# A macaron transformer layer in split fp32: idle-time products, a later normalise, paired copies and an earlier rounding

## The chip, the cores and the metric

The kernel runs on one core of a Trainium2 chip. The time is device time in microseconds from the first to the last instruction of one execution; three executions of the kernel before gave 1914.36, 1914.66 and 1914.83 us (median 1914.66). One further execution was recorded by the profiler: 1912.22 us, of which the trace covers a span of 1910.4 us.

## The reference

One layer of a decoder: a half-step SwiGLU FFN, a token mixer (differential attention beside an S5 state space model), and a second half-step FFN. Each block modulates its input with a shift and a scale that come from a condition vector `c`, and ends in a residual sum and a layer norm. There are 256 tokens, the model width is 2048, all arrays are fp32.

```python
mod = (silu(c) @ w_cond + b_cond)            # 3 blocks x (shift, scale, gate) x 2048
u = x * (1 + scale0) + shift0
h = (silu(u @ w1) * (u @ w3)) @ w2           # first FFN
x = layer_norm(alpha * x + 0.5 * (1 + gate0) * h)
u = x * (1 + scale1) + shift1
q, k, v, s = split(u @ w_in)                 # 4 x 1024 columns
h = concat(diff_attention(q, k, v), s5(s)) @ w_out
x = layer_norm(alpha * x + (1 + gate1) * h)
u = x * (1 + scale2) + shift2
h = (silu(u @ w1b) * (u @ w3b)) @ w2b        # second FFN
x = layer_norm(alpha * x + 0.5 * (1 + gate2) * h)
```

## The kernel before

**Tiles and jobs.** The weights are streamed from DRAM in tiles of 128x1024 fp32. One tile is one job, and the jobs come in a fixed order: 264 of the first FFN, 104 of the mixer (16 s jobs, 32 for q and k, 16 for v, 8 for the gate of the S5 output, 32 of the output product), 264 of the second FFN. Each tile `raw` is split into two rounded parts: `hi` by a cast on ScalarE (line 691), `lo = raw - hi` on VectorE. Activations are split in the same way (`Uh`, `Ul`; `Hh`, `Hl`). TensorE multiplies three times, hi·Uh, hi·Ul and lo·Uh, and adds up in PSUM. A raw tile is loaded by SyncE's queue up to four tiles ahead; `hi` and `lo` have rings of four.

**Order.** The program is written straight through: `Stream.run` emits for each job the products, then what hangs on the job (`post`, and what was put off with `later`), then the split of the tile four jobs on, then `drain`. Each engine works off its own instructions in the order in which they were emitted. `drain` fills VectorE: it keeps a model clock for VectorE (`V.t`) and TensorE (`PE.t`) and emits background work while `V.t` is less than `lim` ahead of `PE.t`. The background work is of two kinds: `gv` steps (one multiply-and-sum of a 128x1024 tile of `w_cond`, 258 of them in all) and the preparation of the S5 tables (`tabc`, `tabr`, `cells`). From job 70 of the first FFN until its end `lim` is 3.0.

**The kosum jobs.** In the first FFN, part of the sums over the input width is kept in SBUF (`kosum`) and completed later; in jobs 70 to 96 VectorE adds these up beside the splitting. From there on a group of up-projection jobs ends with `sg`, the product of silu and the other half, whose transposes TensorE makes next.

**The two turns.** Between blocks, the layer norm is computed per token half t (128 tokens): VectorE gathers the statistics, then `normalise(q)` scales a quarter of 512 columns, on ScalarE for t=0 and on VectorE for t=1 (table `NOW`, all four quarters at once). `turn(ks, then)` transposes Y by TensorE (`ps<-ident,Y`, 128 columns each, twice two for each of the eight pairs `k2`), and `put` makes u from the transposed tile: the scaled copy `uf` and every second `Uh` on ScalarE, the others and `Ul` on VectorE. The first turn covers k2 = 0 and 1, which the first job needs; the others follow one by one between products or jobs. Below, T2 to T7 are the transposes of pairs 2 to 7. T4 and T5 read quarter 2 of Y, T6 and T7 quarter 3.

**The s jobs.** Jobs of the mixer 0 to 7 take half 0 of the input width, 8 to 15 half 1, for the eight tiles t of s. Two tiles share one PSUM buffer. After a job of half 1 ScalarE copies the tile to `sT` (line 1147) and issues its DMA to `sD` in DRAM (line 1150); after t=3 and t=7 GpSimd loads four such tiles back in the layout of the scan (`U<-sD`, line 1156). The scan's first products (`ps<-U,s5e`) come at `S5_AT` = job 17.

Nearly all VectorE and TensorE instructions carry the line of the recording helper (L106), so the rows below are told apart by their tiles.

Of the kernel before, what the change touches and what calls it, by code (L numbers as in the profile page):

```python
# [10 lines left out]
F32R = mybir.dt.float32r  # L11
# [6 lines left out]
T = 256  # L18
# [15 lines left out]
AHEAD = 4  # L34
# [5 lines left out]
LIM = (3.0, 100.0, 100.0, 100.0)  # L40
GVM = (0.57, 0.65, 0.85, 0.4)
LAG = 8.0
S5_WAIT = 1.7
BG_AT = 70
GV_END = 256
GA = (20, 24)
UNITS = ([("p", 0, q) for q in range(4)] + [("g", 2, h) for h in range(2)] + [("p", 3, q) for q in range(4)]
# [2 lines left out]
O_AT = (61, 69)  # L50
H_AT = 21
AV_AT = (57, 65)
S5_AT = 17
S5_STEP = 4
X_AT = (239, 240, 244, 250)
Z_AT = (242, 246, 251, 256)
NOW = (4, 4)
QUIET = 3
RW = (8, 3, 64)
MAGIC = 12582912.0  # L60
# [57 lines left out]
def tile_layer(tc, A, out):  # L118
    nc = tc.nc
    V, S, PE, SP, GP = Meter(nc.vector), nc.scalar, Meter(nc.tensor), nc.sync, nc.gpsimd  # L120
    with ExitStack() as ctx:
        sb = ctx.enter_context(tc.tile_pool(name="sb", bufs=1))
# [7 lines left out]
        def psum():  # L130
            return psp.tile([128, 512], F32, tag="ps", name="ps")
# [7 lines left out]
        def w1(shape, name):  # L139
            return small(shape, name, 5, tag="w1")  # L140
# [16 lines left out]
        SP.dma_start(sc[0:1, :], A["c"])  # L157
        ident = sb.tile([128, 128], F32, tag="ident", name="ident")
        make_identity(nc, ident)
        mask = sb.tile([128, 384], F32, tag="mask", name="mask")  # L160
        GP.memset(mask, 0.0)
        for c0 in (0, 256):
# [27 lines left out]
        for q in range(4):  # L190
            p, cs = psum(), slice(q % 2 * 512, q % 2 * 512 + 512)
# [9 lines left out]
        sD = dram.tile([1024, 4, 64], F32, tag="sD", name="sD")  # L201
        yD = dram.tile([1024, 4, 64], F32, tag="yD", name="yD")

        st = {"raw": RAW, "split": 2, "lim": None, "gv_max": 0.0, "gv_credit": 0.0, "s5_at": 0.0}

        gv_order = [(u, kt) for u in UNITS for kt in range(NS)]
# [22 lines left out]
        def gv_step():  # L231
            n = gv_n["done"]
            gv_load(n + (8 if n < GV_RING else GVB))
            t = gv_tiles.pop(n)
            u, j = gv_order[n]
            if j == 0:
                st["acc"] = small([128, NS], "acc")
                if n < GV_RING:
                    V.memset(st["acc"], 0.0)
            w = t.shape[-1]  # L240
            gv_n["done"] += w // 1024
            if n == 0:
                st["shift"] = p = psum()[:, 0:1]
                for k in range(NK):
                    PE.matmul(p, t[:, k * 128:(k + 1) * 128], scT[:, k:k + 1], start=k == 0, stop=k == NK - 1)
            else:
                c0 = 0 if w > 1024 else j % 2 * 1024
                V.scalar_tensor_tensor(out=t, in0=t, scalar=1.0, in1=sc[:, c0:c0 + w], op0=ALU.mult, op1=ALU.mult,
                                       accum_out=st["acc"][:, j:j + 1])
                pay_late()  # L250
            n, j = gv_n["done"] - 1, j + w // 1024 - 1
            if n < 4 * NS and j % 8 == 7:
                finish(u, st["acc"], j // 4 - 1, j // 4 + 1)
            elif n >= 4 * NS and j == NS - 1:
                gv_end(u, st.pop("acc"))
# [476 lines left out]
        stream = Stream()  # L732
# [146 lines left out]
            for x, n in zip(st["gb"], ("lng", "lnb")):  # L879
                SP.dma_start(x[:, cs], A[n][sub:sub + 1, cs].to_broadcast([128, 1024]))  # L880

        def turn(ks, then):

            ps = {}
            for k2 in ks:
                for t in range(2):
                    st.pop(("norm", k2 // 2, t), lambda: None)()
            for t in range(2):
                for k2 in ks:
                    if t == 0:  # L890
                        ps[k2] = psum()
                    for i in range(2):
                        PE.transpose(ps[k2][:, i * 256 + t * 128:i * 256 + (t + 1) * 128],
                                     st["Y"][t][:, (2 * k2 + i) * 128:(2 * k2 + i + 1) * 128], ident)
                    if t == 1:
                        then(k2, ps[k2])

        def turn_mod(blk):
            def then(k2, p):
                gv_until("ready", blk, k2 // 2)  # L900
                for i in range(2):
                    k = 2 * k2 + i
                    put(kx(st["U"][0], k), kx(st["U"][1], k), p[:, i * T:(i + 1) * T],
                        GS[blk][:, k:k + 1], BT[blk][:, k:k + 1], i)
            return then
# [211 lines left out]
        def mixer():  # L1117
            jobs = []
            M = {}
# [10 lines left out]
            def mk_s(t, hf):  # L1130
                def mm(hi, lo):
                    if hf == 0 and t % 2 == 0:
                        M["ps", t // 2] = psum()
                    M["pt"] = p = M["ps", t // 2][:, (t % 2) * T:(t % 2 + 1) * T]
                    for k in range(8):
                        between(8 * hf + k)
                        w = hi[:, k * 128:(k + 1) * 128]
                        PE.matmul(p, w, kx(st["U"][0], 8 * hf + k), start=hf == 0 and k == 0 and t % 2 == 0,
                                  stop=False, skip_group_check=True)
                        PE.matmul(p, w, kx(st["U"][1], 8 * hf + k), start=False, stop=False, skip_group_check=True)  # L1140
                    for k in range(8):
                        PE.matmul(p, lo[:, k * 128:(k + 1) * 128], kx(st["U"][0], 8 * hf + k), start=False,
                                  stop=hf == 1 and k == 7, skip_group_check=True)

                def post():
                    s = w1([128, 4, 64], "sT")
                    S.copy(s, M["pt"].rearrange("p (c i) -> p i c", i=4))  # L1147
                    if t % 2:
                        M.pop(("ps", t // 2))
                    S.dma_start(sD[t * 128:(t + 1) * 128], s)  # L1150
                    if t % 4 == 3:
                        h = t // 4
                        if h == 0:
                            M["U4"] = slab("U4")
                        for i in range(4):
                            GP.dma_start(
                                M["U4"][32 * i:32 * i + 32, h * 1024:(h + 1) * 1024]
                                .rearrange("p (g c) -> p g c", c=64),
                                sD[h * 512:(h + 1) * 512, i, :].rearrange("(g p) c -> p g c", p=32))
                return Job(mm, halves(A["win_a"][t], hf), post if hf else None)  # L1160
# [392 lines left out]
        stream.q[RW[2]].pre.append(lambda: st.update(raw=RAW))  # L1553
        stream.run(BG_AT)
        bg5.extend(fill)
        n0 = stream.done
        st["gv_due"] = lambda n: 64 + 96.0 * (n - n0) / (GV_END - n0)
        st["lim"], st["gv_max"] = LIM[0], GVM[0]
        stream.run(4 * NT1 - BG_AT)
        bg5.extend(rest)  # L1560
        new_stats()
        stream.run(len(parts[0]) - 4 * NT1 - QUIET)
# [6 lines left out]

        st["X"] = st["Y"]  # L1570
        st["U"] = pairs("U")
        turn(range(2), turn_mod(3))
        mid[2] = lambda: turn((2,), turn_mod(3))
        mid[4] = lambda: turn((3,), turn_mod(3))
        for i in range(4):
# [15 lines left out]
        def kept(k2, p):  # L1591
            q = k2 // 2
            S.copy(xT[:, (k2 % 4) * 512:(k2 % 4 + 1) * 512], p)
            if k2 % 2:
                st["xT", 6, q] = xT[:, (q % 2) * 1024:(q % 2 + 1) * 1024]
                if ("ready", 6, q) in st:
                    modulate(6, q)
        turn(range(2), turn_mod(6))
        stream.later(0, lambda: turn((2,), turn_mod(6)))
        stream.later(1, lambda: turn((3,), turn_mod(6)))  # L1600
        for i in range(4):
# [77 lines left out]
```

## Time and profile before

| | |
|---|---|
| median of three executions | 1914.66 us |
| profiled execution | 1912.22 us, span 1910.4 us |
| TensorE matmuls busy | 1858.5 us, 97% of the span |
| VectorE busy | 1488.1 us, 78% |
| ScalarE busy | 889.4 us, 47% |
| DMA | 532 MB, mean 279 GB/s |
| mean granted clock of TensorE | 0.989 of full speed |

TensorE is the engine to watch: what is not its own work shows up as idle time ahead of a matmul, written in the timeline as `[idle <- what ended it]`. The end of a matmul is modelled, so the distance between two starts tells more than a duration does. The clock column of a window is the mean granted clock in parts of full speed (2.4 GHz); 0.50 is the lower level of 1.2 GHz.

### The profile page before, as it was taken

How to read it: one execution, taken by the hardware profiler on the slowest of the kernel's cores; microseconds unless marked ns; L12 is line 12 of the kernel's file. 1: busy time of each engine (PE TensorE's matmuls, PEld its weight loads, DVE VectorE, ACT ScalarE, POOL GpSimd, SP SyncE). 2: the span in 40 equal slices, each digit the busy share in tenths (PEclk: the TensorE clock that was granted, in tenths of full speed). 3: DMA queues.
4: the chain of work that ended last, by engine and by line, in shares of the span. 5: the costliest groups of instructions: out<-in, count | busy, mean ns of one | idle time of the engine just before them, and what ended most of it. 6: DMA issues, size and time to landing. Idle time of an engine off the chain costs nothing.

```text
span 1910.4 us, 25429 instructions
## 1 busy us (share of the span) xinstructions
PE 1858.5 (97%) x9326; PEld 1567.5 (82%) x9326; DVE 1488.1 (78%) x2255; ACT 889.4 (47%) x1211; POOL 65.0 (3%) x119
## 2 busy tenths in 40 slices
PE   6999999999999999899999998999999999999996
PEld 5888878888888888889999886888888888888885
DVE  6889899978888979888998987887876555445468
ACT  3544444465445433634457635544444444344442
POOL 0000000000000000111210000000000000000000
PEclk9999999999999999999999998999999999999998
DMA  9999878889899888798988885998887555565563
GB/s 375 363 338 315 296 247 292 295 306 309 305 347 326 308 323 312 280 337 294 313 268 311 283 309 202 339 357 275 294 279 249 187 188 191 194 215 187 191 233 110
DMA packets 151935, 532.36 MB, mean 279 GB/s; under 512 B 21841, under 2 KB 23297, under 8 KB 150657
## 3 DMA queue, kind: packets, MB, share of 16 engines
q1 hardware_dynamic: 137234, 495.32, 74.3%
q0 software_dynamic: 6512, 23.89, 3.7%
q10 hardware_dynamic: 8064, 11.54, 1.7%
q8 instruction: 73, 1.20, 0.2%
q14 instruction: 52, 0.43, 0.1%
HBM read 513.34 MB, written 17.33 MB: 278 GB/s over the span
## 4 chain that ended last, share of the span: by engine, by line
PE 87%; DVE 6%; DMA 4%; ACT 2%; issue 1%; POOL 0%; SPq 0%; DVEq 0%; ACTq 0%; POOLq 0%
PE ps L106 87%; DVE lo L106 2%; DVE Y L106 2%; DMA raw<-in_f1w_dram 1%; DVE gv L106 1%; ACT hi L691 1%; DMA early<-in_w_cond_dram 1%; DMA raw<-in_wout_dram 0%; DMA U<-sD 0%; DVE st L106 0%; DVE r L106 0%; DMA sD<-sT 0%; DMA early<-in_wc_dram 0%; ACT Y L865 0%; DVE early L106 0%
## 5 line engine op out<-in xcount | busy, mean ns | idle before, releaser
L106 DVE TENSOR_TENSOR lo<-raw,hi 128x1024 fp32r<-128x1024 f32 x630 | 766.3, 1222 | 342.1 <-ACT hi L691 338.5
L691 ACT CAST hi<-raw 128x1024 fp32r<-128x1024 f32 x630 | 661.4, 1053 | 705.8 <-PE ps L106 461.0
L106 PE MATMUL ps<-hi,Uh 128*128 128x512 f32 x1472 | 583.7, 397 | 16.7 <-ACT Uh L318 9.7
L106 PE MATMUL ps<-hi,Ul 128*128 128x512 f32 x1472 | 577.5, 392 | 0.8 <-DVE Ul L106 0.8
L106 PE MATMUL ps<-lo,Uh 128*128 128x512 f32 x1472 | 457.4, 392 | 1.3 <-DVE lo L106 1.3
L106 PEld LDWEIGHTS ps<-hi,Uh 128*128 128x128 f32 x1472 | 278.7, 189 | 77.8 <-ACT Uh L318 10.4
L106 PEld LDWEIGHTS ps<-lo,Uh 128*128 128x128 f32 x1472 | 278.4, 189 | 60.9 <-DVE lo L106 2.0
L106 PEld LDWEIGHTS ps<-hi,Ul 128*128 128x128 f32 x1472 | 279.0, 190 | 58.1 <-DVE Ul L106 1.9
L106 DVE SCALAR_TENSOR_TENSOR gv<-gv,sc 128x1024 f32<-128x1024 f32 x258 | 314.2, 1219 | 1.4 <-DMA gv<-in_w_cond_dram 1.3
L106 PE MATMUL ps<-hi,Hh 128*128 128x512 f32 (+1 forms) x716 | 274.6, 385 | 0.0
L106 PE MATMUL ps<-hi,Hl 128*128 128x512 f32 (+1 forms) x716 | 273.6, 383 | 0.0
L106 PE MATMUL ps<-lo,Hh 128*128 128x512 f32 (+1 forms) x716 | 216.5, 384 | 1.8 <-DVE lo L106 1.8
L106 PEld LDWEIGHTS ps<-lo,Hh 128*128 128x128 f32 x716 | 133.0, 188 | 29.1 <-DVE lo L106 2.6
L106 PEld LDWEIGHTS ps<-hi,Hh 128*128 128x128 f32 x716 | 134.5, 188 | 26.8 <-issue 0.4
L106 PEld LDWEIGHTS ps<-hi,Hl 128*128 128x128 f32 x716 | 134.6, 188 | 26.0
L106 PE MATMUL ps<-Uh,hi 128*128 128x256 f32 x384 | 97.9, 292 | 2.4 <-ACT sT L1147 1.8
L106 PE MATMUL ps<-Ul,hi 128*128 128x256 f32 x384 | 95.7, 286 | 0.1
L106 PEld LDWEIGHTS ps<-Uh,hi 128*128 128x128 f32 x384 | 74.2, 193 | 6.2 <-ACT sT L1147 2.7
L106 PEld LDWEIGHTS ps<-Ul,hi 128*128 128x128 f32 x384 | 74.2, 193 | 0.8 <-DVE Ul L106 0.7
L1010 ACT CAST Hh<-ps 128x512 fp32r<-128x512 f32 x44 | 25.8, 587 | 78.6 <-PE ps L106 78.6
L106 PE MATMUL ps<-Uh,lo 128*128 128x256 f32 x384 | 53.9, 283 | 0.0
L106 DVE TENSOR_TENSOR Hl<-ps,Hh 128x512 fp32r<-128x512 f32 x44 | 30.3, 688 | 30.0 <-ACT Hh L1010 29.7
(229 smaller groups left out, 1393.4 us busy)
## 6 DMA issues: line engine op xcount, KB each, us to landing
raw<-in_f1w_dram SPq DMA_DIRECT2D x264, 512.0 KB, 6.0
raw<-in_f2w_dram SPq DMA_DIRECT2D x264, 512.0 KB, 4.7
gv<-in_w_cond_dram SPq DMA_DIRECT2D x258, 512.0 KB, 7.1
raw<-in_win_a_dram SPq DMA_DIRECT2D x48, 512.0 KB, 6.0
raw<-in_wout_dram SPq DMA_DIRECT2D x32, 512.0 KB, 5.8
early<-in_w_cond_dram SPq DMA_DIRECT2D x28, 512.0 KB, 7.6
s5m<-scrB POOLq DMA_DIRECT2D x8, 1024.0 KB, 8.4
raw<-in_win_v_dram SPq DMA_DIRECT2D x16, 512.0 KB, 4.8
```

The source lines that it names most:

```text
L106: return f(*a, **k)
L691: S.copy(hi, raw)
L1010: S.copy(hh, p)
```

## The change

- `LIM_KO` = 1.5 takes the place of 3.0 as `lim` for jobs 70 to 96; after these it is 3.0 as before.
- `S5_AT` is 18 in place of 17: the scan's loads and products come one job later.
- `NOW` = (4, 1): for t=1, VectorE normalises only quarter 0 at once. Quarter 1 follows right behind the first turn, quarters 2 and 3 at the start of the turns of T4 and T6.
- `warm(n)` emits n products 128x512 of a small constant tile `wr` into a PSUM buffer that nobody reads: 20 after the first shift product at the opening; 11 after the t=0 transposes and 3 after the t=1 transposes of the mixer's first turn; 12 and 3 at the second FFN's.
- The s copies wait for the odd tile and are then made for both.
- In the second FFN, `split_to(done + AHEAD, False)` right behind the first turn emits the casts of the next three tiles there.

```diff
@@ constants
+LIM_KO = 1.5
-S5_AT = 17
+S5_AT = 18
-NOW = (4, 4)
+NOW = (4, 1)
+WARM = dict(opening=20, mixer=(11, 3), ffn=(12, 3))
@@ tile_layer
+        wr = sb.tile([128, 32], F32R, tag="wr", name="wr")
+        V.tensor_copy(wr, ident[:, 0:32])
...
+        def warm(n):
+
+            p = psum()
+            for _ in range(n):
+                PE.engine.matmul(p, wr[:, 0:1].to_broadcast([128, 128]), wr.unsqueeze(1).to_broadcast([128, 16, 32]), start=True, stop=True)
...
                     PE.matmul(p, t[:, k * 128:(k + 1) * 128], scT[:, k:k + 1], start=k == 0, stop=k == NK - 1)
+                warm(WARM["opening"])
@@ turn
-        def turn(ks, then):
+        def turn(ks, then, idle=(0, 0)):
...
                     if t == 1:
                         then(k2, ps[k2])
+                if idle[t]:
+                    warm(idle[t])
@@ mk_s
                 def post():
-                    s = w1([128, 4, 64], "sT")
-                    S.copy(s, M["pt"].rearrange("p (c i) -> p i c", i=4))
-                    if t % 2:
-                        M.pop(("ps", t // 2))
-                    S.dma_start(sD[t * 128:(t + 1) * 128], s)
+                    if t % 2 == 0:
+                        return
+                    p = M.pop(("ps", t // 2))
+                    for i in range(2):
+                        s = w1([128, 4, 64], "sT")
+                        S.copy(s, p[:, i * T:(i + 1) * T].rearrange("p (c i) -> p i c", i=4))
+                        S.dma_start(sD[(t - 1 + i) * 128:(t + i) * 128], s)
                     if t % 4 == 3:
@@ main program
-        st["lim"], st["gv_max"] = LIM[0], GVM[0]
+        st["lim"], st["gv_max"] = LIM_KO, GVM[0]
         stream.run(4 * NT1 - BG_AT)
+        st["lim"] = LIM[0]
         bg5.extend(rest)
...
-        turn(range(2), turn_mod(3))
+        turn(range(2), turn_mod(3), WARM["mixer"])
+        st.pop(("norm", 1, 1))()
         mid[2] = lambda: turn((2,), turn_mod(3))
...
-        turn(range(2), turn_mod(6))
+        turn(range(2), turn_mod(6), WARM["ffn"])
+        st.pop(("norm", 1, 1))()
+        stream.split_to(stream.done + AHEAD, False)
         stream.later(0, lambda: turn((2,), turn_mod(6)))
```

VectorE near the end of the first FFN's up-projections, before: the second S5 table is finished here (`tabc<-tabc,tabr 128x16x32` are its last two operations), and then there are only splits and `gv` steps.

```order
L106 TENSOR_TENSOR lo<-raw,hi 128x1024
L106 SCALAR_TENSOR_TENSOR gv,acc<-gv,sc 128x1024
L106 TENSOR_TENSOR tabc<-tabc,tabr 128x16x32
L106 TENSOR_TENSOR lo<-raw,hi 128x1024
L106 SCALAR_TENSOR_TENSOR gv,acc<-gv,sc 128x1024
L106 TENSOR_TENSOR lo<-raw,hi 128x1024
L106 TENSOR_TENSOR tabc<-tabc,tabr 128x16x32
L106 TENSOR_TENSOR lo<-raw,hi 128x1024
L106 SCALAR_TENSOR_TENSOR gv,acc<-gv,sc 128x1024
L106 TENSOR_TENSOR lo<-raw,hi 128x1024 x2
```

The same last operations in the changed program. The first `lo` of this piece is split 241 of the stream; in the piece above the first is split 231.

```order
L108 TENSOR_TENSOR lo<-raw,hi 128x1024
L108 SCALAR_TENSOR_TENSOR gv,acc<-gv,sc 128x1024
L108 TENSOR_TENSOR tabc<-tabc,cells 128x32x32
L108 TENSOR_TENSOR lo<-raw,hi 128x1024
L108 TENSOR_TENSOR tabr<-tabc,cells 128x1024
L108 TENSOR_TENSOR lo<-raw,hi 128x1024
L108 SCALAR_TENSOR_TENSOR gv,acc<-gv,sc 128x1024
L108 TENSOR_TENSOR sg<-sg,ps 128x512 x2
L108 TENSOR_TENSOR lo<-raw,hi 128x1024
L108 TENSOR_TENSOR tabc<-tabc,tabr 128x16x32
L108 TENSOR_TENSOR lo<-raw,hi 128x1024
L108 SCALAR_TENSOR_TENSOR gv,acc<-gv,sc 128x1024
```

The last table operations have moved some ten splits later, past the last `sg` of the up-projections.

VectorE at the mixer's first turn, before, from the four normalises of t=1 (`Y<-Y,mv,rs`) on; the last `CAST Uh` here belongs to T4.

```order
L106 TENSOR_SCALAR Y<-Y,mv,rs 128x512 x4
L106 CAST Uh<-uf 128x256
L106 TENSOR_TENSOR Ul<-uf,Uh 128x256 x2
L106 CAST Uh<-uf 128x256
L106 TENSOR_TENSOR Ul<-uf,Uh 128x256 x2
L106 TENSOR_TENSOR lo<-raw,hi 128x1024
...
L106 TENSOR_TENSOR lo<-raw,hi 128x1024 x4
L106 SCALAR_TENSOR_TENSOR gv,acc<-gv,sc 128x1024
L106 CAST Uh<-uf 128x256
```

The same stretch in the changed program; the third normalise is that of quarter 2, which T4 reads.

```order
L108 TENSOR_SCALAR Y<-Y,mv,rs 128x512
L108 CAST Uh<-uf 128x256
L108 TENSOR_TENSOR Ul<-uf,Uh 128x256 x2
L108 CAST Uh<-uf 128x256
L108 TENSOR_TENSOR Ul<-uf,Uh 128x256 x2
L108 TENSOR_SCALAR Y<-Y,mv,rs 128x512
L108 TENSOR_TENSOR lo<-raw,hi 128x1024
...
L108 TENSOR_TENSOR lo<-raw,hi 128x1024 x4
L108 SCALAR_TENSOR_TENSOR gv,acc<-gv,sc 128x1024
L108 TENSOR_SCALAR Y<-Y,mv,rs 128x512
L108 CAST Uh<-uf 128x256
```

Three of the four normalises have moved back; quarter 2 now stands behind four splits and a `gv` step, and quarter 3 two splits and another `gv` step further on.

VectorE at the second FFN's first turn in the changed program, from the normalise of quarter 1 to that of quarter 2 and the `gv` step behind it. Before, a single `lo` stood ahead of T2's `CAST Uh` here, four behind it, and no normalise among them.

```order
L108 TENSOR_SCALAR Y<-Y,mv,rs 128x512
L108 TENSOR_TENSOR lo<-raw,hi 128x1024 x4
L108 CAST Uh<-uf 128x256
L108 TENSOR_TENSOR Ul<-uf,Uh 128x256 x2
L108 TENSOR_TENSOR lo<-raw,hi 128x1024
L108 CAST Uh<-uf 128x256
L108 TENSOR_TENSOR Ul<-uf,Uh 128x256 x2
L108 TENSOR_TENSOR lo<-raw,hi 128x1024
L108 SCALAR_TENSOR_TENSOR gv,acc<-gv,sc 128x1024
L108 TENSOR_SCALAR Y<-Y,mv,rs 128x512
L108 TENSOR_TENSOR lo<-raw,hi 128x1024
L108 SCALAR_TENSOR_TENSOR gv,acc<-gv,sc 128x1024
```

The four splits have come forward past T2's put, and the normalise of quarter 2 stands behind a split and a `gv` step.

## Rows read from the trace of the kernel before

**Rows 1.** page, chain that ended last: share of the span by engine
```profile
PE 87%; DVE 6%; DMA 4%; ACT 2%; issue 1%; POOL 0%; SPq 0%; DVEq 0%; ACTq 0%; POOLq 0%
```

**Rows 2.** TensorE's waits: us in total, times, longest
```profile
PE ps L106 <- ACT Uh L318: 9.7, 2, 7.6
PE ps L106 <- DVE Y L106: 6.3, 2, 3.2
...
PE ps L106 <- DVE kosum L106: 3.3, 3, 1.2
...
PE ps L106 <- ACT sT L1147: 1.8, 4, 0.5
```

**Rows 3.** timeline, TensorE at the opening: start, us, engine, operation, [idle before]
```profile
38.86 0.74 PE L106 MATMUL ps<-hi,Uh 128*128 128x512 f32 x1 [2.09 <-ACT Uh L318]
```

**Rows 4.** timeline, VectorE in a kosum period
```profile
266.75 1.28 DVE L106 TENSOR_TENSOR kosum<-ps,kosum 128x512 f32<-128x512 f32 x2
```

**Rows 5.** timeline, VectorE in the last up-projections and TensorE beside it
```profile
712.69 1.22 DVE L106 TENSOR_TENSOR lo<-raw,hi 128x1024 fp32r<-128x1024 f32 x1 [2.15 <-ACT hi L691]
...
718.75 1.28 DVE L106 TENSOR_TENSOR sg<-sg,ps 128x512 f32<-128x512 f32 x2
...
720.26 0.60 PE L106 MATMUL ps<-ident,sg 128*128 128x128 f32 x4
...
773.97 0.72 PE L106 MATMUL ps<-lo,Hh 128*128 128x512 f32 x2 [1.20 <-DVE lo L106]
```

**Rows 6.** windows: length, busy PE, PEld, DVE, ACT, POOL, clock, DMA
```profile
714.00:774.00 60.00, 58.80 (x276) 48.83 (x274) 58.68 (x84) 25.55 (x25) 0.00 (x0) 1.00 0.85 303
787.50:792.50 5.00, 4.42 (x19) 3.85 (x17) 4.61 (x12) 4.11 (x9) 2.05 (x4) 0.50 0.98 353
1152.50:1167.50 15.00, 10.86 (x26) 7.74 (x27) 8.73 (x15) 7.25 (x12) 0.00 (x0) 0.50 0.20 66
```

**Rows 7.** timeline, VectorE and TensorE at the start of the mixer
```profile
786.11 2.04 DVE L106 TENSOR_SCALAR Y<-Y,mv,rs 128x512 f32<-128x512 f32 x4
788.07 0.28 DVE L106 CAST Uh<-uf 128x256 fp32r<-128x256 f32 x1
...
795.01 4.64 DVE L106 TENSOR_TENSOR lo<-raw,hi 128x1024 fp32r<-128x1024 f32 x4 [0.52 <-ACT hi L691]
799.57 1.22 DVE L106 SCALAR_TENSOR_TENSOR gv<-gv,sc 128x1024 f32<-128x1024 f32 x1
...
802.60 1.22 DVE L106 TENSOR_TENSOR lo<-raw,hi 128x1024 fp32r<-128x1024 f32 x1
...
786.71 1.11 PE L106 MATMUL ps<-ident,Y 128*128 128x128 f32 x4 [3.06 <-DVE Y L106]
...
798.60 0.60 PE L106 MATMUL ps<-ident,Y 128*128 128x128 f32 x4
...
805.23 0.60 PE L106 MATMUL ps<-ident,Y 128*128 128x128 f32 x4
```

**Rows 8.** timeline, the s tiles' way to the scan: ScalarE's queue, GpSimd, TensorE
```profile
831.17 0.33 ACTq L1150 DMA_DIRECT2D sD<-sT  x1
...
838.16 2.59 POOL L1156 DMA_DIRECT2D U<-sD  x4 [46.89 <-ACT sT L1147]
...
848.87 1.97 PE L106 MATMUL ps<-U,s5e 128*128 128x64 f32 x16 [2.30 <-DMA U<-sD]
```

**Rows 9.** timeline, TensorE and ScalarE at the start of the second FFN
```profile
1156.25 1.22 PE L106 MATMUL ps<-lo,Uh 128*128 128x512 f32 x2 [1.27 <-DVE lo L106]
...
1163.38 0.79 PE L106 MATMUL ps<-hi,Uh 128*128 128x512 f32 x1 [2.49 <-ACT hi L691]
...
1169.07 0.47 PE L106 MATMUL ps<-hi,Uh 128*128 128x512 f32 x1
...
1178.33 0.60 PE L106 MATMUL ps<-ident,Y 128*128 128x128 f32 x4
...
1162.29 3.88 ACT L691 CAST hi<-raw 128x1024 fp32r<-128x1024 f32 x4
```

More of the change, by code (lines that the diff above doesn't have):

```diff
@@ L1133, in mm @@
                         M["ps", t // 2] = psum()
-                    M["pt"] = p = M["ps", t // 2][:, (t % 2) * T:(t % 2 + 1) * T]
+                    p = M["ps", t // 2][:, (t % 2) * T:(t % 2 + 1) * T]
                     for k in range(8):
```

## The prediction

> **What bounds the kernel now.** The chain of waits comes first: 87% of it is TensorE [rows 1], so the kernel is bound by the products, and only time in which TensorE stands still or runs at the lower clock can be gained. The list of TensorE's waits then says how much there is: 9.7 us in two waits for ScalarE's Uh, 6.3 in two for VectorE's Y, 3.3 in three for kosum, 1.8 in four for the sT copy [rows 2]. Each is followed up in the timeline, engine beside engine, and the granted clock is read in windows around them. The lower level of 1.2 GHz (0.50) holds for 5 us at the mixer's start and for 15 us at the second FFN's [rows 6]. Every part of the change touches one of these places, and each is small: their sum is what decides.
>
> **The opening.** The 20 unread products stand in the first long wait, 7.6 us [rows 2]. What one costs comes from the second FFN: from 1163.38 to 1169.07 lie 13 times 512 columns, 0.44 us each at the lower level; from 1169.07 to 1178.33 lie 38, 0.24 each [rows 9]. Twenty take 4.9 to 8.8 us, so at worst they end 1.2 late. What would be gained by a faster clock behind them is lost again: after jobs 0 to 3 TensorE waits 2.09 us for the next Uh [rows 3], which hangs on loads and conditions and not on TensorE. The same wait hides the 1.2. Value 0, bounds -0.8 (the waits behind 2.09 shrink a little) and +1.2.
>
> **LIM_KO.** Each kosum wait ends on the sum at 266.75 [rows 4], which stands behind a lo and a gv step. The order of the changed kernel keeps that gv step and takes away the one of the earlier split, where VectorE isn't late. I take 0.1 of the 3.3 us; bounds 0 and 3.3. What is deferred comes back later: the last four table operations now stand behind splits 241, 242, 244 and 245. At VectorE's durations for such sizes, 1.22 for 1024 elements (the lo rows) and 0.64 for 512 (two sg in 1.28) [rows 5], they are 2 x 1.22 + 2 x 0.64 = 3.7 us. Before them VectorE has idle time, as the 2.15 at 712.69 shows [rows 5]. Behind them it has not: from 714 to 774 it is busy for 58.7 of 60 us [rows 6], and TensorE ends that stretch waiting 1.20 for lo [rows 5]. So 3.7 less the 1.3 idle, +2.4, appears there, part of it already at 720.26, where the transposes start 0.2 to 0.3 behind the end of sg [rows 5]. Bounds: 0, if VectorE had got further ahead by then, and 3.7. The part: +2.3.
>
> **The mixer's turn.** The four normalises took 2.04 us from 786.11, and the first CAST Uh followed at 788.07 [rows 7]. But that CAST also needs ScalarE's uf, which needs the transposes at 786.71; at best it starts 1.3 us after these, so hardly earlier than now. The later normalising gains 0.1 here. What is late next are T2, T4 and T6. T2 reads quarter 1, which now stands behind the first four Ul: about 0.4 net, since ScalarE's puts are the pace there. T4 was reached at 798.60. Quarter 2 stands behind the four lo from 795.01 and the gv step from 799.57, and takes 2.04 / 4 = 0.51: 799.57 + 1.22 + 0.51 = 801.3, a new wait of 2.7 us. T6 was reached 6.63 us after T4. VectorE needs between T4 and T6: 1.36 until the CAST (from 786.71 to 788.07), 1.9 for the put and the small operations (from the gv step's end near 800.7 to 802.60), a lo of 1.16, a gv step of 1.22, a put of some 1.2, a lo of 1.16 and the normalise of 0.51, in all 8.5 [rows 7]. That is 1.9 of new wait. Eleven products of 0.24 fill 2.7 of the 3.06 us at 786.71, so the clock may stay up there instead of at 0.50 for 5 us; but that stretch goes at the pace of the puts, VectorE 4.61 and ScalarE 4.11 busy of 5.00 [rows 6], and I take 0.5 for it. Together -0.1 + 0.4 + 2.7 + 1.9 - 0.5 = +4.4. Bounds +1.5 (T6 not late, a full gain of the clock) and +7 (the clock falls in the new wait of 2.7, as it did in the one of 3.06, and costs half of another 5 us).
>
> On this point the Trainium skill (Perfetto Trace Analysis, the part on how TensorE's profile differs) says that ScalarE, VectorE and GpSimd are strictly first in, first out. By that rule the normalise cannot pass the lo and gv rows, and the two waits stand; were it otherwise, the part would be about 0 and the sum 4.6 us lower.
>
> **The s tiles.** TensorE waited four times 0.45 for a copy of the tile whose buffer it needed [rows 2]; with copies only after the odd tile the next job has another buffer: -1.8. The loads of the scan: sD is issued at 831.17, GpSimd issues U from 838.16, TensorE waits 2.30 until 848.87 [rows 8]. Now one more copy and issue stand ahead, 0.45 + 0.33 = 0.8 later; TensorE gets there a job later, half of 6.63 less a turn's 0.4 [rows 7], 2.9 us, less the two waits of 0.45 that vanish in between. The wait becomes 2.30 + 0.8 - 2.9 + 0.9 = 1.1: -1.2. Together -3.0; bounds -1.8 and -4.1.
>
> **The second FFN's turn.** Job 1 started at 1163.38 after 2.49 us for a hi whose casts ScalarE began only at 1162.29 [rows 9]. Now three are cast before. The first lo, awaited until 1156.25, moves back by one normalise, to 1156.75. From there job 0 has 8 products and T2 left, 9 x 512 columns: at 0.24 to 0.44 each job 1 starts at 1158.9 to 1160.7, and job 2 (13 x 512 on) at 1162.1 to 1166.4, where it was at 1169.07 [rows 9]: a gain of 7.0 at full clock, 2.7 at the lower level, 5.6 if the clock comes back early in job 1. The last is what I take, since TensorE still stands 2.75 us before 1156.75. Then T4: from T3 on, ScalarE needs 1.7 for the put (1.36 to VectorE's CAST [rows 7], and its own last cast) and 3.88 / 4 = 0.97 for the hi, VectorE 1.16 + 1.22 + 0.51, in all 5.6 against 13 x 0.24 = 3.2: a new wait of 2.4. T6 stands behind lo, gv, lo, gv: 1.7 by the same sums. Together -5.6 + 2.4 + 1.7 = -1.5; bounds -4.5 and +1.5.
>
> **The sum.** 0 + 2.3 + 4.4 - 3.0 - 1.5 = +2.2 us on the profiled execution of 1912.2 us, 1914.4. The median of the runs lies 2.4 above that execution, so 1916.9; with the clock's side a little kinder in both turns than the middle of my bounds, I put down 1916.5.
>
> **Rivals.**
> 1. *The clock is the main thing.* The products keep 2.4 GHz through both turns: the 15 us at 0.50 [rows 6] hold 10.9 us of matmul, of which half, 5.4, comes back, 7.0 with the earlier start; the mixer gives back 2.2 of its 4.42. The new waits are shorter because VectorE is ahead: 3.5 in all for T4 and T6 of both turns. -3.0 - 7.0 - 2.2 + 3.5 + 1.0 (tables) = -7.7: about 1907. For it: the gap of 3.06 is nearly filled. Against it: the puts set the pace, and the new waits are as long as some that stood before. The Trainium skill (TensorE: Matmul & The Clock Gate, "What's actually happening") has the low level as the default that activity lifts; by it the unread products should hold the clock, which the rows of the kernel before can't show, as nothing fills the gaps there.
> 2. *The late normalises lower the clock again.* The new waits of 2.7 and 2.4 at T4 each drop it, as the one of 3.06 ahead of 786.71 was followed by 0.50 [rows 6, 7]. Against it: after the wait of 2.30 the 16 products of 64 columns took 1.97 us [rows 8], no sign of a lower level, and the new waits lie between the two. It decides once the windows behind T4 show 0.50 at all. Price 2.5 each, half of the mixer's 5 us: +2.2 + 5.0, on the scale of the median 1922.
> 3. *The shorter limit does what it says.* The three kosum waits go and the tables find room: -3.3 - 2.3 instead of +2.3: 2.2 - 5.5, about 1911.
>
> **Chances.** The forecast, with a spread of 3 us, 0.50; rival 1 0.18; rival 2 0.20; rival 3 0.12. The measurement tells about 0.2%, 3.8 us, from no change: faster is below 1910.8, slower above 1918.5. Faster: 0.16 of rival 1, 0.05 of rival 3, 0.03 of the forecast, 0.24. Slower: 0.18 of rival 2 and 0.11 of the forecast, 0.29. The same: 0.47. The range of 8 in 10 leaves out the lower half of rival 1 and the upper half of rival 2: 1908 to 1922.
>
> **What will show it.** Idle times ahead of the transposes of T4 and T6 in both turns, ended by VectorE's Y: 2.7, 1.9, 2.4, 1.7. No wait for sT and one near 1.1 for U. Waits for sg or lo near 720 and 774 that are 2.4 us longer in sum. The kosum waits still 3 and 3.2 us. Job 1 of the second FFN near 1159 relative to the lo that ends the wait of 1156. I am wrong if T4 starts without a wait, if the windows of the turns show a clock near 1.00 throughout with TensorE the pace, or if VectorE's tables fit before 714.

## The result, and the profile after

The changed kernel takes 1924.45 us (median of six executions, 1919.88 to 1930.91) against 1914.74 for the kernel before, measured beside it: a ratio of 1.0051, 95% interval 1.0031 to 1.0070, so 6 to 13 us slower. The forecast was 1916.5. Single executions of one kernel lie up to 8 us from their median (1907.36 to 1919.64 around 1914.87 in 26 executions of the kernel before), so times below come with their interval, and a single trace is read for where the time goes.

The profiled execution of the changed kernel, the fastest of its six, has a span of 1918.1 us. The page's chain of waits, which was 87% TensorE before [rows 1]:

```profile
PE 80%; DVE 9%; DMA 5%; ACT 3%; issue 2%; ACTq 1%; POOL 0%; SPq 0%; DVEq 0%
```

TensorE's share fell by seven points, VectorE's rose from 6% to 9%. The list of TensorE's waits (total, times, longest):

```profile
PE ps L108 <- DVE Y L108: 9.9, 7, 2.4
PE ps L108 <- DVE lo L108: 6.0, 4, 2.5
PE ps L108 <- ACT Uh L329: 4.8, 2, 4.0
...
PE ps L108 <- DVE kosum L108: 3.2, 3, 1.1
PE ps L108 <- DMA U<-sD: 3.1, 1, 3.1
PE ps L108 <- DVE s5e L108: 2.6, 3, 1.4
```

The waits for sT are gone and the opening's waits for Uh have shrunk from 9.7 to 4.8 us [rows 2], as the 20 unread products now stand in the first of them. Waits for Y have grown from two to seven, for lo from 3.6 to 6.0 us in sum, and there are three for s5e that did not stand there before. The timeline of TensorE shows the places, each with the idle time ahead:

```profile
38.29 0.50 PE L108 MATMUL ps<-hi,Uh 128*128 128x512 f32 x1 [3.96 <-ACT Uh L329]
...
755.86 0.73 PE L108 MATMUL ps<-lo,Hh 128*128 128x512 f32 x2 [0.80 <-DVE lo L108]
...
773.25 0.73 PE L108 MATMUL ps<-lo,Hh 128*128 128x512 f32 x2 [1.94 <-DVE lo L108]
...
790.71 0.44 PE L108 MATMUL ps<-ident,Y 128*128 128x128 f32 x2 [1.25 <-DVE Y L108]
...
801.27 0.44 PE L108 MATMUL ps<-ident,Y 128*128 128x128 f32 x2 [2.32 <-DVE Y L108]
...
809.49 0.44 PE L108 MATMUL ps<-ident,Y 128*128 128x128 f32 x2 [1.38 <-DVE Y L108]
...
853.77 2.43 PE L108 MATMUL ps<-U,s5e 128*128 128x64 f32 x16 [3.11 <-DMA U<-sD]
...
999.74 0.77 PE L108 MATMUL ps<-s5e,s5m 128*128 128x64 f32 x4 [1.39 <-DVE s5e L108]
...
1164.76 0.72 PE L108 MATMUL ps<-lo,Uh 128*128 128x512 f32 x2 [2.46 <-DVE lo L108]
...
1177.43 0.44 PE L108 MATMUL ps<-ident,Y 128*128 128x128 f32 x2 [2.38 <-DVE Y L108]
...
1185.56 0.44 PE L108 MATMUL ps<-ident,Y 128*128 128x128 f32 x2 [1.48 <-DVE Y L108]
```

At 38.29 the opening's second wait is 3.96 us in place of 2.09 [rows 3]: what the earlier jobs gained is waited off here. 755.86 and 773.25 are lo waits near the end of the first FFN, 2.7 us in place of 1.20 [rows 5]. 790.71, 801.27 and 809.49 are T2, T4 and T6 of the mixer, 1177.43 and 1185.56 T4 and T6 of the second FFN. 853.77 is the scan's first product, 999.74 a product of a later batch of the scan.

To see where the time went, the trace is cut at instructions that both kernels have: the first kosum transposes, the first transposes of the mixer's turn, T7, the scan's first product, the first transposes of the second FFN's turn, its T7, the last product. In us, from one trace of each kernel:

| stretch | before | changed | difference |
|---|---|---|---|
| start to kosum | 247.9 | 246.3 | -1.6 |
| kosum to the mixer's turn | 535.2 | 536.0 | +0.9 |
| the mixer's turn, to T7 | 25.5 | 30.3 | +4.9 |
| T7 to the scan's first product | 40.3 | 41.1 | +0.8 |
| scan's first product to the second FFN's turn | 298.6 | 301.9 | +3.3 |
| the second FFN's turn, to T7 | 34.1 | 32.9 | -1.2 |
| T7 to the last product | 714.5 | 715.2 | +0.7 |

The fourth and fifth stretch belong together, because the scan begins one job (2.9 us) later: together +4.1.

The granted clock in windows (third number from the end; the first five pairs are the busy times of TensorE, its weight loads, VectorE, ScalarE, GpSimd):

```profile
787.50:792.50 5.00, 3.49 (x19) 2.15 (x17) 4.58 (x10) 3.42 (x8) 1.81 (x4) 1.00 0.97 329
800.00:805.00 5.00, 3.73 (x32) 3.73 (x33) 3.60 (x14) 2.38 (x4) 0.00 (x0) 1.00 0.89 267
853.00:855.50 2.50, 1.73 (x14) 1.76 (x15) 0.85 (x3) 1.05 (x1) 0.00 (x0) 0.92 1.03 414
855.50:858.00 2.50, 2.50 (x13) 2.50 (x13) 0.61 (x1) 0.00 (x0) 1.86 (x3) 0.50 1.03 419
858.00:860.50 2.50, 2.50 (x21) 2.50 (x20) 0.13 (x1) 1.05 (x1) 1.28 (x3) 0.90 1.02 413
1002.50:1005.00 2.50, 2.50 (x8) 2.03 (x8) 2.43 (x7) 0.48 (x3) 0.00 (x0) 0.50 0.95 277
1165.00:1167.50 2.50, 2.50 (x8) 1.83 (x8) 2.50 (x3) 0.49 (x1) 0.00 (x0) 0.65 0.64 179
```

In the mixer's turn the clock now stays at 1.00 where it was 0.50 [rows 6], also behind the wait of 2.32 (800 to 805). Behind the 3.11 us for U it falls to 0.50, behind the 1.39 us for s5e to 0.50 (1002.5 to 1005), and behind the 2.46 us for lo in the second FFN to 0.65.

### The profile page after: what moved, and what is told of

Read it like the earlier page. It is cut to its first block, busy times and chain, and to the rows that moved or that the text cites. A ratio compares the mean times of both kernels' runs of the same rounds, so it can differ in the third digit from the quotient of the medians.

```text
span 1918.1 us, 25529 instructions
## 1 busy us (share of the span) xinstructions
PE 1868.0 (97%) x9375; PEld 1572.9 (82%) x9375; DVE 1490.2 (78%) x2256; ACT 889.4 (46%) x1211; POOL 65.0 (3%) x119
## 4 chain that ended last, share of the span: by engine, by line
PE 80%; DVE 9%; DMA 5%; ACT 3%; issue 2%; ACTq 1%; POOL 0%; SPq 0%; DVEq 0%
PE ps L108 80%; DVE lo L108 3%; DMA raw<-in_f1w_dram 2%; DVE Y L108 1%; DVE gv L108 1%; ACT hi L702 1%; DMA gv<-in_w_cond_dram 1%; ACTq L1273 1%; ACT pr L1342 1%; DMA early<-in_w_cond_dram 1%; DMA raw<-in_f2w_dram 1%; DMA U<-sD 1%; DMA raw<-in_win_a_dram 0%; DVE sa L108 0%; DVE mx L108 0%
## 5 line engine op out<-in xcount | busy, mean ns | idle before, releaser
L108 PEld LDWEIGHTS ps<-lo,Hh 128*128 128x128 f32 x716 | 132.8, 188 | 31.6 <-DVE lo L108 5.2
L108 PEld LDWEIGHTS ps<-hi,Hl 128*128 128x128 f32 x716 | 134.6, 188 | 26.1
```

Source lines behind the costliest of these rows:

```text
L108: return f(*a, **k)
```

## The experiments

Each was timed against the kernel before on the same chip. "Changed" is the changed kernel. The kernel before had medians of 1914.74 to 1915.9 us beside the different experiments. Where two intervals of the table overlap, the times alone don't show a difference between the two kernels; there the stretches of the traces are the firmer evidence.

| kernel | median us | ratio to before, 95% interval |
|---|---|---|
| changed | 1924.45 | 1.0051 (1.0031 to 1.0070) |
| changed, batches at 17 | 1923.83 | 1.0050 (1.0036 to 1.0064) |
| before, batches at 18 | 1914.92 | 1.0003 (0.9991 to 1.0016) |
| changed, softmax at 22 | 1918.40 | 1.0023 (1.0009 to 1.0037) |
| before, paired copies | 1916.03 | 1.0011 (0.9999 to 1.0024) |
| changed, y issued by GpSimd | 1920.57 | 1.0027 (1.0016 to 1.0038) |
| changed, all normalises at once | 1912.69 | 0.9985 (0.9977 to 0.9994) |
| changed, no unread products | 1924.20 | 1.0045 (1.0033 to 1.0057) |
| changed, limit 3.0 | 1920.71 | 1.0026 (1.0014 to 1.0037) |
| combination | 1901.68 | 0.9930 (0.9918 to 0.9943) |
| combination, no unread products | 1902.07 | 0.9938 (0.9925 to 0.9952) |
| combination, no earlier rounding | 1907.60 | 0.9957 (0.9943 to 0.9970) |
| combination, products before the scan | 1903.15 | 0.9939 (0.9927 to 0.9952) |

### The scan's place: four experiments on one cause

The stretch from the scan's first product to the second FFN was the largest surprise, and the waits for s5e lie in it. What stands there on ScalarE is best seen around one batch. Before (ScalarE, ACTq its queue of DMA issues):

```profile
977.19 0.37 ACT L1256 COPY y<-ps 128x256 f32<-128x256 f32 x1 [3.50 <-PE ps L106]
977.60 2.21 ACTq L1258 DMA_DIRECT2D yD<-y  x4
979.85 1.05 ACT L691 CAST hi<-raw 128x1024 fp32r<-128x1024 f32 x1 [2.28 <-DMA yD<-y]
...
981.06 0.41 ACT L1327 ACTIVATE pr<-pr,nb 128x128 f32<-128x128 f32 x1
```

A batch's y is copied (977.19) and issued in four DMAs (2.21 us), then comes the hi cast, and the four exponentials of a head begin only behind it at 981.06. The changed kernel:

```profile
986.64 0.40 ACT L1342 ACTIVATE pr<-pr,nb 128x128 f32<-128x128 f32 x1 [3.68 <-DVE nb L108]
...
988.42 0.35 ACT L1271 COPY y<-ps 128x256 f32<-128x256 f32 x1
988.80 2.29 ACTq L1273 DMA_DIRECT2D yD<-y  x4
991.13 1.05 ACT L702 CAST hi<-raw 128x1024 fp32r<-128x1024 f32 x1 [2.36 <-issue]
```

Here the exponentials come first (from 986.64), then y, then its four issues, and only at 991.13 the hi cast. VectorE waits for that hi: over the scan's 140 us, 19.4 us in 8 places, up to 5.5,

```profile
DVE lo L108 <- ACT hi L702: 19.4, 8, 5.5
```

where it was 13.0 in 12, at most 2.2, before:

```profile
DVE lo L106 <- ACT hi L691: 13.0, 12, 2.2
```

**Batches back at job 17.**

```diff
-S5_AT = 18
+S5_AT = 17
```

> The changed kernel with the scan's batches back at job 17 (S5_AT = 17), all else as changed. Phase theory: at job 18 each batch's y copy and its four DMA issues stand right behind the four exponentials of a head on ScalarE, the next hi cast comes some 2.3 us late, and VectorE's lo and s5e are late for TensorE (three waits for s5e, 2.6 us, and a fall of the clock behind one). At 17 these are apart again: no wait for s5e, and between the scan's first product and the end of the mixer 4 to 6 us less than the changed kernel; the wait for U grows by one job, 2.9, from 3.1 to about 6. Sum 2 to 3 us faster than changed, about 1921 to 1922. Late-U theory (the longer way of the s tiles alone makes the scan stage late): waits for s5e stay or grow, and the time is 3 us or more above the changed kernel, 1927.

Measured: no wait for s5e, as the phase theory has it, but no gain in time either, 1923.83. The wait for U is 5.32 us, and behind it the clock stays low:

```profile
857.00:859.50 2.50, 2.33 (x11) 2.36 (x12) 0.30 (x2) 0.00 (x0) 0.00 (x0) 0.50 1.03 417
859.50:862.00 2.50, 2.50 (x13) 2.50 (x13) 0.00 (x0) 0.00 (x0) 2.21 (x4) 0.50 1.03 419
862.00:864.50 2.50, 2.50 (x13) 2.50 (x13) 0.00 (x0) 0.00 (x0) 0.92 (x2) 0.50 1.06 352
```

Three windows of 0.50, each 1.25 us of full clock: together with the longer wait, TensorE gave back there what the batches gained (T7 to the second FFN 342.0 us, changed 343.1). So S5_AT = 18 is bad and, with the rest of the change, 17 is as bad; the late-U theory had a part of it.

**The kernel before with batches at job 18.**

```diff
-S5_AT = 17
+S5_AT = 18
```

> The kernel before with the scan's batches at job 18 and nothing else. Phase theory: the wait for U (2.3) vanishes, but waits for s5e appear (2 to 3 us in three or more places) with a fall of the clock: 2 to 5 us slower than before, 1917 to 1920. Late-U theory: U is in time, nothing else changes, 2.3 us faster than before, about 1912.5.

Measured: 1.0003 (0.9991 to 1.0016), no change. The trace has both halves of the phase theory:

```profile
851.56 1.63 PE L106 MATMUL ps<-U,s5e 128*128 128x64 f32 x13 [0.65 <-DMA U<-sD]
...
978.81 0.77 PE L106 MATMUL ps<-s5e,s5m 128*128 128x64 f32 x4 [0.86 <-DVE s5e L106]
...
995.83 0.77 PE L106 MATMUL ps<-s5e,s5m 128*128 128x64 f32 x4 [1.69 <-DVE s5e L106]
```

The wait for U shrinks to 0.65, and two waits for s5e, 2.6 us, appear. From T7 to the second FFN this one trace is 4.4 us longer than before (343.4 against 338.9), which the timed runs, at most +3.1, don't bear out in full: the 2 to 5 us that the phase theory expected are not shown in the median. How large the loss is when this edit stands alone stays open.

**Softmax one job later too.**

```diff
-H_AT = 21
+H_AT = 22
```

> The changed kernel with the heads' softmax moved one job later too (H_AT = 22), which puts exponentials and y copies at the distance that they had before. Phase theory: no wait for s5e, U still awaited for about 3.1 with the fall of the clock behind it; 4 to 5 us faster than changed, about 1919.5 to 1920.5. Late-U theory: the waits for s5e stay, no change from the changed kernel.

Measured: 1918.4, 6 us below the changed kernel (the two intervals overlap), no wait for s5e left, and 296.4 us from the scan's first product to the second FFN in place of 301.9. The late-U theory had no change here; it falls as the main cause.

**y issued by GpSimd.**

```diff
-                        S.dma_start(yD[b * 128:(b + 1) * 128, i, :].rearrange("(g p) c -> p g c", p=32),
+                        GP.dma_start(yD[b * 128:(b + 1) * 128, i, :].rearrange("(g p) c -> p g c", p=32),
```

> The changed kernel with the four DMA issues of each batch's y on GpSimd's queue in place of ScalarE's; batches at 18 and softmax at 21 as changed. Issue theory: it is the 2.2 us of issues between the exponentials and the next hi cast on ScalarE that make lo and s5e late: no wait for s5e, and from the scan's first product to the second FFN's turn about 297 us, as with the softmax a job later (296.4), in place of 302; 4 to 6 us faster than the changed kernel, about 1919.5. Crowding theory (exponentials, VectorE's softmax and the batch's own steps fall into one job, whoever issues the DMAs): the waits for s5e stay and the stretch stays above 300, within 2 us of the changed kernel.

Measured: 1920.57, 3.9 us below the changed kernel (the two intervals overlap); the stretch takes 297.8 us, and no wait for s5e is left. ScalarE around a batch:

```profile
987.61 0.40 ACT L1342 ACTIVATE pr<-pr,nb 128x128 f32<-128x128 f32 x1
...
989.97 0.37 ACT L1271 COPY y<-ps 128x256 f32<-128x256 f32 x1 [0.50 <-PE ps L108]
990.24 1.05 ACT L702 CAST hi<-raw 128x1024 fp32r<-128x1024 f32 x1
```

The hi cast follows 0.27 us behind the start of the y copy and not 2.7. The exponentials still stand directly ahead of it, so it was the issues that made lo late. The issue theory holds; of the 5.5 us that the softmax's move is worth in this stretch, the issues explain 4.1. It is not one trace against one: the five traces with the batches at 18, the softmax at 21 and the issues on ScalarE take 301.8 to 303.7 us there, the five with the softmax at 22 take 294.8 to 298.2.

### Paired copies alone

```diff
                 def post():
-                    s = w1([128, 4, 64], "sT")
-                    S.copy(s, M["pt"].rearrange("p (c i) -> p i c", i=4))
...
+                    if t % 2 == 0:
+                        return
+                    p = M.pop(("ps", t // 2))
+                    for i in range(2):
...
```

> The kernel before with the s tiles copied out in pairs and nothing else (batches at job 17). Both theories: the four waits for sT (1.8 us) go; the way of the third and fourth tile gets longer by one copy and one issue (0.8) and TensorE gets there 0.9 earlier: the wait for U grows from 2.3 to 4 or more. If that longer wait is followed by a lower clock, as the 3.1 of the changed kernel is (0.50 to 0.92 for 7 us), it is 2 us slower than before, about 1917; if not, the same as before, 1914.7.

Measured: 1.0011 (0.9999 to 1.0024): between no change and 4.6 us slower. The waits for sT went, and TensorE was ready for the scan's first product 35.1 us after T7 where it had been 38.0. The wait for U stayed at 2.34 all the same (expected 4 or more), because in this trace, the fastest of twelve executions, it took 15.5 us from the issue of the fourth s tile to the first product. Before it took 17.7, and in ten traces of the changed kernel and its variants 18.4 to 19.5. What the paired copies do to a wait for U at job 17 with such a way is seen above: 5.32. This time the clock fell behind 2.34:

```profile
845.19 1.08 PE L106 MATMUL ps<-U,s5e 128*128 128x64 f32 x8 [2.34 <-DMA U<-sD]
...
845.19:847.69 2.50, 2.50 (x17) 2.50 (x18) 1.07 (x1) 1.59 (x2) 0.00 (x0) 0.78 1.01 365
847.69:850.19 2.50, 2.50 (x14) 2.50 (x14) 2.50 (x5) 0.50 (x1) 0.76 (x2) 0.54 1.02 393
```

(0.22 x 2.5 and 0.46 x 2.5 us: 1.7 us of full clock lost.) After almost the same wait, 2.30, the kernel before kept 1.00. A wait of this size is followed by either.

### The normalises

```diff
-NOW = (4, 1)
+NOW = (4, 4)
...
-        st.pop(("norm", 1, 1))()
...
-        st.pop(("norm", 1, 1))()
```

> The changed kernel with all four quarters of the second token half normalised at once again (NOW = (4, 4)); the unread products, the earlier rounding and all else stay. Late-normalise theory: the five waits for Y at T2, T4 and T6 of both turns go (1.25, 2.32, 1.38, 2.38, 1.48 in the changed kernel, 8.8 in sum), the first Uh of each turn comes about 0.3 later: 7 to 8 us faster than the changed kernel, about 1917. Pace theory (ScalarE's puts and VectorE's lo set the pace, and the waits for Y only stand where others would): waits of the same size for Uh, lo or uf appear, 0 to 3 us faster, 1921 to 1924.

Measured: 1912.69, 11.8 us below the changed kernel, more than the 7 to 8 expected, and 0.9985 of before. Little took the place of the waits for Y: 1.1 us in three waits for VectorE's Uh, and 6.6 us for lo where it was 6.0. The mixer's turn takes 25.0 us in place of 30.3, the second FFN's 28.2 in place of 32.9: together 10.0 of the 11.8; where the rest comes from is not shown. The pace theory falls.

### Without the unread products

```diff
-WARM = dict(opening=20, mixer=(11, 3), ffn=(12, 3))
+WARM = dict(opening=0, mixer=(0, 0), ffn=(0, 0))
...
-                warm(WARM["opening"])
+                if WARM["opening"]:
+                    warm(WARM["opening"])
```

> The changed kernel without any unread product. Clock theory: without them the granted clock goes back to 0.50 for some 5 us at the mixer's turn and 8 to 15 at the second FFN's, and job 1 there starts later: 3 to 6 us slower than the changed kernel, 1927 to 1930, and the opening 1.5 us slower. Puts-set-the-pace theory, as the prediction had it: the clock falls but the stretches are no longer, within 1 us of the changed kernel, 1924.

Measured: 1924.20, no change. The clock did fall, all through the mixer's turn:

```profile
789.00:791.50 2.50, 1.94 (x8) 1.31 (x7) 1.20 (x4) 1.98 (x5) 1.01 (x2) 0.50 0.96 296
...
794.00:796.50 2.50, 2.50 (x12) 2.26 (x11) 1.69 (x5) 2.21 (x5) 1.32 (x3) 0.50 0.96 340
```

and TensorE was the slower for it, but the wait at T4 took most of that up. Here T4 is 804.75, T6 812.97:

```profile
804.75 0.44 PE L108 MATMUL ps<-ident,Y 128*128 128x128 f32 x2 [0.68 <-DVE Y L108]
...
812.97 0.44 PE L108 MATMUL ps<-ident,Y 128*128 128x128 f32 x2 [1.38 <-DVE Y L108]
```

0.68 in place of 2.32 at T4; T6 waits 1.38 as with the products. The turns take 31.5 and 34.2 us, which lies within the 30.3 to 31.6 and 32.9 to 34.4 of the five traces with late normalises and products. The clock theory falls in the changed kernel, and in the combination too, where no late normalise is in the way (1902.07 against 1901.68, expected 3 to 6 us more):

> The faster version (normalises at once, limit 3.0, softmax at 22, paired copies, earlier rounding) without any unread product. Clock theory: with the late normalises gone the clock matters: 0.50 comes back for 5 us in the mixer's turn and 10 us or more in the second FFN's, 3 to 6 us slower than with them, about 1905 to 1907.5. Puts-set-the-pace theory: within 1.5 us, about 1902.

In that pair the second FFN's turn takes 28.8 us without and 28.2 with the products, the mixer's 25.3 and 26.1, and the start to kosum 248.4 and 250.1. The products cost and gain nothing that these runs can tell; a difference of 3 us would not have shown.

### The limit

```diff
-LIM_KO = 1.5
+LIM_KO = 3.0
```

> The changed kernel with the limit at 3.0 all through the first FFN (LIM_KO = 3.0). Table theory: the S5 table is done ten splits earlier, the waits for lo near the end of the first FFN (0.80 and 1.94) fall back to one of 1.2, a wait of 0.4 to 0.5 for s5w and one for sg come back: 0.5 to 1.5 us faster than the changed kernel, 1923 to 1924. Limit theory: the three waits for kosum grow, and it is 2 us slower.

Measured: 1920.71, 3.7 us below the changed kernel (the two intervals overlap). From kosum to the mixer's turn, the eight traces with 3.0 take 533.7 to 535.2 us, mean 534.4, the six with 1.5 take 536.0 to 538.3, mean 536.9: 2.5 us for the shorter limit. The kosum waits are 3.2 and 3.3 us. The waits for sg are back as expected (two, 0.9 us), that for s5w is not in the list, and of the lo waits 2.9 us are left, most of it the second FFN's 2.46. The limit theory falls.

### The combination

The costs taken out, the rest kept:

```diff
-LIM_KO = 1.5
+LIM_KO = 3.0
-H_AT = 21
+H_AT = 22
-NOW = (4, 1)
+NOW = (4, 4)
...
-        st.pop(("norm", 1, 1))()
...
-        st.pop(("norm", 1, 1))()
```

> The changed kernel with what cost taken out: NOW = (4, 4), LIM_KO = 3.0, and the heads' softmax a job later (H_AT = 22) so that it keeps its distance from the scan's batches at 18; the unread products, the paired copies and the earlier rounding stay. If the costs add: the changed kernel less 8 (late normalises), 5 (phase) and 1 (tables), about 1910.5, 4 us faster than before. If they overlap: 1914 to 1917, no better than before.

Measured: 1901.68, ratio 0.9930 (0.9918 to 0.9943): 11 to 16 us faster than before and 23 below the changed kernel, more than the 14 us that were expected if the costs add. What remains at the second FFN's turn:

```profile
1151.66 0.66 PE L108 MATMUL ps<-ident,Y 128*128 128x128 f32 x4 [0.23 <-DVE Y L108]
...
1156.60 1.06 PE L108 MATMUL ps<-lo,Uh 128*128 128x512 f32 x2 [1.95 <-DVE lo L108]
```

The transposes of t=1 wait 0.23 us where it was 3.23 before, as twelve unread products stand ahead of them; the first lo is awaited for 1.95, before for 1.27 [rows 9].

**Without the earlier rounding.**

```diff
-        stream.split_to(stream.done + AHEAD, False)
```

> The faster version without the three casts ahead in the second FFN's turn. Rounding theory: job 1 waits 2.5 us or more for hi again and with that wait the clock falls: from the second FFN's first transposes to its last turn (T7) 33 to 34 us in place of 28.2, 4 to 6 us slower, about 1906 to 1907.5. Clock theory (the unread products alone shorten that stretch): within 2 us, 1902 to 1904.

Measured: 1907.60, 5.9 us slower (the two intervals just touch). Job 1 waits for hi as it did before [rows 9],

```profile
1161.43 0.72 PE L108 MATMUL ps<-hi,Uh 128*128 128x512 f32 x1 [2.49 <-ACT hi L702]
```

and the turn takes 32.6 us in place of 28.2. The four traces with the rounding and all normalises at once take 28.2 to 28.8, the three of the kernel before and its edits, without the rounding, 32.8 to 34.1. The rounding theory holds.

**Products before the scan.**

```diff
                 def enter():
+                    if b == 0:
+                        warm(11)
```

> The faster version with eleven unread products more, ahead of the scan's first product, where TensorE stands 3 us for U and the clock falls to 0.5 behind it (windows 0.76 and 0.56). Clock theory: the clock stays at 1.00 there, 1.5 to 2 us faster, about 1900. Rival: the stretch behind is bound by VectorE and ScalarE, no change within 1 us, or the products end after U has landed and it is 0.3 us slower.

Measured: 1903.15, no difference that can be told from the combination's 1901.68. The clock did stay up behind the scan's first product,

```profile
846.00:848.50 2.50, 2.50 (x22) 2.35 (x21) 1.09 (x3) 1.04 (x1) 0.02 (x1) 1.00 1.03 418
```

and in this trace the stretch from T7 to the second FFN is 335.2 us in place of 337.4. The timed runs don't show these 2 us; whether they are there stays open.

## Why the prediction was wrong

The sum was +2.2 us and the result is +9.7 (6 to 13); on the profiled executions +7.7. By its own parts:

- **The opening**, 0: right. The nine traces with the products reach kosum after 249.0 us on average, the five without after 248.8. In the profiled execution the second wait grew by 1.9 us, which is where the gain went.
- **LIM_KO**, +2.3: right in size (2.5 by fourteen traces, though +0.9 in the table's pair) and in place (lo waits near 756 and 773). Rival 3, that the kosum waits go, was wrong: 3.2 us as before.
- **The mixer's turn**, +4.4: right, a little small. The waits at T4 and T6 were put at 2.7 and 1.9 and measured 2.32 and 1.38; T2, put at 0.4, waited 1.25. The turn is 4.9 us longer in this trace; over all traces 30.9 with late normalises against 25.2 without, 5.7.
- **The s tiles**, -3.0: this is the step that failed. Measured +4.1. Two of its terms were mis-sized, and the largest was put at nothing.

  The four sT waits were taken at their idle time, 4 x 0.45 = 1.8. From start to start each cost 0.72, 2.9 in all: ScalarE's copies of the first three tiles start at 820.68, 824.29 and 827.16 before, 6.48 us for two jobs, and in the changed kernel the first two pairs start at 827.66 and 833.42, 5.76 for two jobs. This much was gained.

  The wait for U, "1.1", was 3.11, longer than before by 0.8. TensorE is earlier by the larger worth of two sT waits (0.5), and from the issue of the fourth tile to the first product it took 19.1 us, where it had been 17.7 [rows 8]: 7.4 in place of 7.0 until GpSimd's issue, and 11.8 in place of 10.7 from there (the changed kernel):

```profile
834.63 0.33 ACTq L1165 DMA_DIRECT2D sD<-sT  x1
...
841.98 2.59 POOL L1171 DMA_DIRECT2D U<-sD  x4 [51.03 <-DMA raw<-in_win_a_dram]
```

Behind that wait the clock fell, 1.7 us more. These three make -2.9 + 0.8 + 1.7 = -0.4. The other 4.5 us, a fall of the clock behind s5e among them, were never priced: the step counted what the move of the batches does to their first load, and nothing of what the eight batches issue, one every four jobs. Their y copies and DMA issues on ScalarE moved past the exponentials of the heads, in front of a hi cast. Putting the softmax a job later takes 5.5 us out of this stretch, taking the issues off ScalarE 4.1.

- **The second FFN's turn**, -1.5: -1.2 in this pair of traces. But the three traces of the kernel before and its edits (32.8 to 34.1, mean 33.6) and the five of the changed kernel and its variants with late normalises and products (32.9 to 34.4, mean 33.5) don't differ, so a gain is not shown. The earlier rounding was put at 5.6; it is 4.4 in the trace and 5.9 in time. The late normalise was put at 2.4 + 1.7 and its waits measured 2.38 and 1.48.

Rival 1, that the clock is the main thing, was wrong: the products held it through the profiled mixer's turn, and the time without them is the same within the intervals. The forecast's sentence on strict order in VectorE was borne out: both waits that hang on it stood there.

Rival 2, that the waits at T4 lower the clock again, is not refuted. In the profiled execution the clock stayed at 1.00 behind both, and fell behind the waits for U, s5e and lo. In other traces it fell behind T4, as here with the limit at 3.0 (T4 of the mixer):

```profile
802.03 0.44 PE L108 MATMUL ps<-ident,Y 128*128 128x128 f32 x2 [2.33 <-DVE Y L108]
...
802.00:804.50 2.50, 2.47 (x15) 2.47 (x16) 1.22 (x4) 1.96 (x4) 0.00 (x0) 0.67 0.83 246
```

The six traces with late normalises have ten waits of 2.27 to 2.58 us at T4 of the two turns; behind five of them the clock fell to 0.50, behind five it stayed at 1.00. The cost is under the 2.5 us that the rival put on it: the turn above takes 31.2 us, the two without any fall 30.3. Whether executions of the changed kernel other than the profiled one had such falls stays open. The rival's time, 1922, came nearest.

What the median shows beyond the profiled execution (+9.7 against +7.7) is within the scatter of single executions.

## What to carry to other kernels

When a periodic step is moved by one job, list for every engine what it issues in each period and what stands next to it there, DMA issues on a compute engine's queue above all; here the first occurrence was the smaller part of the price (2.5 us of wait and clock, against 4.5 for the rest). Price a wait from start to start and not by its idle time: the sT waits showed 0.45 and cost 0.72 each. An instruction moved from a place where its wait was hidden costs what is queued ahead of it at the new place: here a 0.5 us normalise made TensorE wait 2.3 to 2.4. Holding TensorE's clock through a turn brought nothing that could be measured here, where other engines set the pace of that turn; look for the wait (here a cast that could stand 8 us earlier) before the clock.

## What the runs showed of the hardware that was not expected

- The clock can be held in a gap, though not always: with unread products in it, it stayed at 1.00 from 787.5 to 792.5 in the changed kernel, where it had been 0.50. In three of the nine traces with products (y issued by GpSimd, softmax at 22, the combination) it fell to 0.50 all the same, 9 to 11 us behind the first transposes of the mixer's turn.
- Waits of about the same length end differently: behind 2.30 us (before) and 2.32 us (changed, T4) the clock stayed at 1.00, behind 2.34 us (paired copies alone) and 2.33 us (limit 3.0, T4) it fell to 0.54 and 0.67 in windows of 2.5 us. Even at one place it goes either way: T4 of the mixer waited 2.32 us in the changed kernel and 2.27 us with the softmax at 22, and the clock stayed in the first and fell to 0.54 in the second.
- Four small DMA issues keep ScalarE's queue busy for 2.2 to 2.3 us, twice as long as the hi cast (1.05) that stands behind them.
- The way of a tile from ScalarE's issue through DRAM to the product that reads it took 15.5 to 19.5 us in these traces, so a wait at its end says little from one trace.
